# A hybrid attention and RWKV block on one core: the loads of the first norm reordered, the constants' broadcast copies spread, and a tile of its own for the last group's operand sums

## The chip, the cores and the metric

The kernel runs on one core of a Trainium2 chip. The metric is the device time of one execution in microseconds (us); the time before is the median of three runs. The core has a matrix engine (TensorE, PE in the profile), VectorE (DVE), ScalarE (ACT), GpSimd (POOL) and SyncE (SP), which here only issues DMA transfers. Each engine works through a queue of its own in order and waits on semaphores for the others. Operands lie in an on-chip memory of 128 partitions; TensorE writes to eight PSUM banks of 2 KB per partition. The language puts the instructions into the queues itself: a planner walks through the program with a cost model, and of the instructions that it takes to be ready puts first the one that comes first in the program. An order can be pinned by hand: `queue_behind(a, b)` sets a behind b in the queue of their engine, `keep_in_program_order(a)` sets a behind the instruction that the program has just before it on its engine; neither adds a wait.

## The reference, cut to what matters

One layer over 2048 rows of 1024 numbers, float32:

```python
h = rms_norm(x, pre_mix_g)
proj = h @ w_in                      # columns for attention q/k/v, RWKV r/k/v + low-rank w/a/g, gates
y_a = chunk_band_attention(q, k, v, rel_bias)     # own chunk of 64 and 8 chunks before, learned bias
y_b = rwkv7_time_mix(p_rwkv, shift_mu, w0, w2, a0, a2, g2, ...)
merged = sigmoid(gate_a) * (y_a @ proj_a) + sigmoid(gate_b) * (y_b @ proj_b)
x = x + rms_norm(merged @ w_out, post_mix_g)
u = square(relu(rms_norm(x, pre_ffn_g) @ w_up)) @ w_down
x = x + rms_norm(u, post_ffn_g)
```

## The kernel before, in words

Products keep float32 accuracy with operands in two parts: `split` (L69) rounds a tile to the matrix engine's format on ScalarE (hi, the "cast" below) and takes the rest on VectorE (lo, L71); `mm3` (L74) then issues three matmuls for each block of 128 in the contraction: hi by hi, hi by lo, lo by hi. Here whi and wlo are the weights' parts, hh and hl those of the normed rows.

The rows are taken in four groups of 512 (`G`), each of four tiles of 128 (`GT`). `run` (L1416) first starts the constants (memsets, identity), then the norm of group 0 in `phase_norm` (L285), then the rest of the constants, and then for each group `phase_rwkv`, `phase_attention` and `phase_merge`; after that the feed-forward part runs in two halves.

The norm of a tile (`norm_tile`, L315): a square with a sum on ScalarE (L319), the root in two steps on GpSimd (`rstd`, L102), a scale by root and gain on VectorE (L321), eight 128 by 128 transposes on TensorE into two PSUM banks, and from each bank a cast on ScalarE (L130) and a low part on VectorE (L131). The pool of these banks has two buffers. The program has the gain (g_pre) loaded ahead of the rows x. The order of the four tiles' steps on each engine is the planner's.

The second part of `constants` (from L199) loads the small parameter rows (L203) and the low-rank weights (L210), transposes the rows on TensorE (L212), splits the low-rank weights, and calls `build_bias` (L950). That one loads the relative biases, extends them on VectorE (ext), writes them to DRAM (band, L961), and copies the band of each of eight heads 128 times into DRAM with a shifted row length (skew, eight copies of 384 KB, L963); attention later reads its bias tiles from there. Eight further small copies (x0, L229) fill the start value of the inverse in RWKV. All of them are issued by SP.

A dense product of 128 columns (`dense`, L93) loads its 512 KB of weights over SP (`wsplit`, L58; two raw buffers), splits them, and issues 24 matmuls of 128 by 512. In group 0 the first is block 12 (`lora_wa`), the next are blocks 0, 4 and 8, that is r, k and v of the first pair of heads (`rwkv_pre`, L377). `rwkv_pre` calls `between()` at eight places, where the products of the gates are put in; `bias_corners` (L974) then overwrites corners of skew.

In `phase_merge` (L1044) eight products of the attention output are gated and added (th, mb), and then `w_out` is applied: two halves n, in each eight blocks k over four tiles t, which end in four PSUM banks ps_o; each bank is squared on ScalarE (L1080) and scaled into o on VectorE (L1081). Beside the first half run the steps of a generator (`beside`), one at each of k = 2, 4, 5, 6, 7: the load of four 256 KB tiles cmb (L1149), four subtractions in place on VectorE (L1121), and the stores (wd, L1145). These are operand sums for the feed-forward part. `run` puts cmb into a pool p1, ahead of the pools p0 and mo (o, g_post, sqo).

After the last group `mixing` is closed, and its memory goes to the feed-forward pools in the order z, b, raw and so on. `first_half` (L1161) loads bl (L1166) and splits it into bh and bl; `phase_up` follows. A tile that takes the memory of an earlier one waits for the last use of that one.

Of the kernel before, what the change touches and what calls it, by code (L numbers as in the profile page):

```python
# [9 lines left out]
F32 = mybir.dt.float32  # L10
# [3 lines left out]
ALU = mybir.AluOpType  # L14
# [36 lines left out]
class Block:  # L51
# [5 lines left out]

    def wsplit(self, src, tag, k, n, raw_tag="raw", bufs=2):  # L58

        nc = self.nc  # L60
        w = self.wp
        raw = w.tile([P, k, n], F32, tag=raw_tag, name="wraw")
        nc.sync.dma_start(raw, src)
        hi = w.tile([P, k, n], F32R, tag=tag + "h", bufs=bufs, name="whi")
        lo = w.tile([P, k, n], F32R, tag=tag + "l", bufs=bufs, name="wlo")
        self.split(hi, lo, raw)
        return hi, lo

    def split(self, hi, lo, src):  # L69
        high = self.nc.scalar.copy(hi, src)  # L70
        self.nc.vector.tensor_tensor(lo, src, hi.bitcast(F32), ALU.subtract)  # L71
        return high.ins

    def mm3(self, ps, terms):  # L74

        nc = self.nc
        n, last, mm = 0, 3 * len(terms) - 1, []
        for lh, ll, rh, rl in terms:
            for l, r in ((lh, rh), (lh, rl), (ll, rh)):
                mm.append(nc.tensor.matmul(ps, l, r, start=n == 0, stop=n == last).ins)  # L80
                n += 1
        return mm
# [5 lines left out]
    def blocks_behind(self, *places):  # L88

        for ins, i in zip(self.blocks, places):  # L90
            self.queue_behind(ins, self.mm[i])

    def dense(self, col):  # L93

        wh, wl = self.wsplit(
            self.a["w_in"][:, col : col + P].rearrange("(k p) n -> p k n", p=P), "w", KB, P
        )
        ps = self.pd.tile([P, G], F32, tag="d", name="psd")
        self.mm = self.mm3(ps, [(wh[:, k], wl[:, k], self.h[0][:, k], self.h[1][:, k]) for k in range(KB)])
        return ps  # L100

    def rstd(self, pool, ssq, scale, eps, post=None):  # L102
        nc = self.nc
        v = pool.tile([P, 1], F32, tag="rs_v", bufs=4, name="rs_v")
        nc.gpsimd.tensor_scalar(v, ssq, scale, eps, ALU.mult, ALU.add)
        r = pool.tile([P, 1], F32, tag="rs_r", bufs=4, name="rs_r")
        nc.gpsimd.tensor_tensor(r, v, self.nhalf[:, 0:1], ALU.pow)  # L107
# [11 lines left out]
    def transpose_split(self, pt, src, hi, lo, tok, pinned=False):  # L119

        nc = self.nc
        for h in range(2):
            ps = pt.tile([P, 4, P], F32, tag="tr", name="pstr")
            for j in range(4):
                k = h * 4 + j
                mm = nc.tensor.transpose(ps[:, j], src[:, k * P : (k + 1) * P], self.ident)
                if pinned and j == 0:
                    self.tc.keep_in_program_order(mm)
            hv, lv = hi[:, h * 4 : h * 4 + 4, tok], lo[:, h * 4 : h * 4 + 4, tok]
            nc.scalar.copy(hv, ps)  # L130
            nc.vector.tensor_tensor(lv, ps, hv.bitcast(F32), ALU.subtract)  # L131


    def constants(self, ctx, mixing):
# [57 lines left out]
        with tc.tile_pool(name="setup", bufs=1, side="right") as sp, \  # L192
# [18 lines left out]
            ps = pp.tile([P, nrow], F32, name="ps_rows")  # L211
            nc.tensor.transpose(ps, raw, self.ident[:nrow, :nrow])  # L212
            nc.vector.tensor_copy(self.cst, ps)

            for par in range(2):
                r = slice(par * C, par * C + C)
                nc.scalar.copy(self.wh[par], raw2[par])
                o = slice(C - par * C, P - par * C)
                nc.vector.memset(self.wl[par][o].bitcast(F32), 0.0)
                nc.vector.tensor_tensor(  # L220
                    self.wl[par][r], raw2[par][r], self.wh[par][r].bitcast(F32), ALU.subtract
                )
            self.build_bias(sp, dp)
            eyeb = sp.tile([2, 512], BF16, name="eyeb")
            nc.vector.tensor_copy(eyeb, eye.rearrange("p r j -> p (r j)"))
            eyed = dp.tile([2, 512], BF16, name="eyed")
            nc.sync.dma_start(eyed, eyeb)
            for i in range(8):
                nc.sync.dma_start(  # L229
                    self.x0[i * 16 : i * 16 + 16].rearrange("p r j -> p (r j)"),  # L230
                    eyed[i % 2][None, :].to_broadcast((16, 512)),
                )

# [50 lines left out]

    def phase_norm(self, g, sp, pt, ahead=2):  # L285

        self.h = self.alloc_h()
        gt = self.gain(sp, self.a["pre_mix_g"], "g_pre", ahead if ahead == 2 else 1)
        for t in range(GT):
            x = sp.tile([P, D], F32, tag="x", bufs=ahead, name="x")  # L290
            self.nc.sync.dma_start(x, self.a["x"][g * G + t * P : g * G + (t + 1) * P])
            self.norm_tile(sp, pt, x, gt, *self.h, slice(t * P, (t + 1) * P), ahead)
            yield

# [20 lines left out]
    def norm_tile(self, sp, pt, x, gt, hi, lo, tok, ahead=2, pinned=False):  # L315
        nc = self.nc
        xn = sp.tile([P, D], F32, tag="xn", bufs=ahead, name="xn")
        ssq = sp.tile([P, 1], F32, tag="ssq", bufs=4, name="ssq")
        nc.scalar.activation(xn, x, AF.Square, accum_out=ssq)  # L319
        r = self.rstd(sp, ssq, 1.0 / D, RMS_EPS)  # L320
        nc.vector.scalar_tensor_tensor(xn, x, r, gt, op0=ALU.mult, op1=ALU.mult)  # L321
        self.transpose_split(pt, xn, hi, lo, tok, pinned)


# [391 lines left out]
    def phase_rwkv(self, g, quads):  # L716
        tc = self.tc
        with ExitStack() as ctx:
# [230 lines left out]

    def build_bias(self, sp, dp):  # L950

        nc = self.nc

        self.skew = dp.tile([8, P * 769], F32, name="skew")
        band = dp.tile([8, 768], F32, name="band")
# [3 lines left out]
        nc.vector.tensor_scalar(ext[:, 383:703], ext[:, 383:703], -1.0, None, ALU.mult)  # L959
        nc.vector.tensor_copy(ext[:, 0:383], ext[:, 383:384].to_broadcast((8, 383)))  # L960
        nc.sync.dma_start(band, ext)  # L961
        for h in range(8):
            nc.sync.dma_start(  # L963
                self.skew[h].rearrange("(q m) -> q m", m=769)[:, 0:768], band[h][None, :].to_broadcast((P, 768))
            )

    def load_bias(self, h):
# [76 lines left out]
    def phase_merge(self, g, o, op, between, beside):  # L1044

        tc, nc, a = self.tc, self.nc, self.a
        with ExitStack() as ctx:
# [13 lines left out]
            for n in range(2):  # L1061
                ps = [po.tile([P, 512], F32, tag="o", name="ps_o") for _ in range(GT)]
                for k in range(KB):
# [3 lines left out]
                    for t in range(GT):  # L1067
                        ts = slice(t * P, (t + 1) * P)
                        for j, (l, r) in enumerate(((mh, wh), (mh, wl), (ml, wh))):
                            nc.tensor.matmul(  # L1070
                                ps[t], l[:, k, ts], r[:, k % 2], start=k == 0 and j == 0, stop=k == KB - 1 and j == 2
                            )
                    if n == 0 and k in (2, 4, 5, 6, 7):
                        advance(beside, 1)
# [341 lines left out]
    def run(self):  # L1416
        tc, e = self.tc, None
        with ExitStack() as ctx, ExitStack() as mixing:
# [90 lines left out]
```

## Time and profile before

| what | value |
|---|---|
| median of 3 runs | 3300.28 us (3299.59 to 3302.99) |
| profiled execution | 3302.74 us, of it the span from first to last instruction 3301.0 us |
| TensorE busy | 3189.4 us, 97% of the span |
| VectorE, ScalarE, GpSimd busy | 68%, 48%, 18% |
| transfers | 592.53 MB, 179 GB/s over the span |
| granted TensorE clock, mean | 0.992 |

How to read it: a row of the timeline gives start and length in us, engine, line, operation, the tile written, an arrow, the tiles read, shapes, and in brackets how long the engine stood idle before it and who ended that. SPq and POOLq stand for issuing a transfer, not for the transfer. A row of the waits gives who waited, for whom, the total in us, how often, and the longest. A row of the windows gives a stretch, then for each of PE, PEld (weight load), DVE, ACT and POOL the busy time, then the granted clock, the share of time in which the transfer engines were busy, and GB/s.

### The profile page before, as it was taken

To read this page: it belongs to the slowest core of one execution; us is meant where nothing else is said; L and a number is where in the kernel's file an instruction comes from. 1 tells how busy PE (TensorE), PEld (TensorE's weight loads), DVE (VectorE), ACT (ScalarE), POOL (GpSimd) and SP (SyncE) were. 2 spreads that over 40 slices of the span, in tenths; PEclk is the share of its full clock that TensorE was granted. 3 is DMA by queue.
4 is the path that set the end of the run, shared out by engine and by line. 5 is a ranking of instruction groups with operands and counts; after the bars stand their busy time and mean duration, and the time that the engine had idled before them with its cause. 6 is when DMAs were issued, how large, how long until landed. Compare 5 with 4: busy or idle time off the path is not lost. (4 is left out here: it accounts for less than half of the span.)

```text
span 3301.0 us, 49967 instructions
## 1 busy us (share of the span) xinstructions
PE 3189.4 (97%) x18913; PEld 2601.3 (79%) x18913; DVE 2245.6 (68%) x3655; ACT 1570.8 (48%) x2511; POOL 595.8 (18%) x1093
## 2 busy tenths in 40 slices
PE   7999999999999999999999999999999999999998
PEld 5777778778877777878777887878788878888887
DVE  5875766785766875776876775777656667775455
ACT  3434634434744434754444654544543454454343
POOL 2222012222102222111232110122211112220000
PEclk9999999999999999999999999999999999999999
DMA  5335473247564236555326647654787875546665
GB/s 152 90 110 185 129 239 118 81 131 240 170 223 150 87 108 222 189 194 185 96 76 201 200 155 234 231 179 153 248 291 239 285 248 190 170 161 235 193 215 178
DMA packets 432281, 592.53 MB, mean 179 GB/s; under 512 B 25300, under 2 KB 295840, under 8 KB 432040
## 3 DMA queue, kind: packets, MB, share of 16 engines
q1 hardware_dynamic: 375080, 413.14, 40.0%
q0 software_dynamic: 47744, 159.42, 13.1%
q10 hardware_dynamic: 9216, 16.78, 1.4%
q8 instruction: 149, 2.44, 0.3%
q14 instruction: 92, 0.75, 0.1%
HBM read 425.37 MB, written 167.01 MB: 179 GB/s over the span
## 5 line engine op out<-in xcount | busy, mean ns | idle before, releaser
L1345 PE MATMUL ps_dn<-fop 128*128 128x512 f32 x2688 | 611.8, 389 | 2.9 <-DVE fop L71 2.9
L1345 PEld LDWEIGHTS ps_dn<-fop 128*128 128x128 f32 x2688 | 503.9, 188 | 108.9 <-DVE fop L71 4.3
L80 PE MATMUL psd<-hh,whi 128*128 128x512 f32 x1344 | 541.4, 403 | 10.7 <-ACT whi L70 7.0
L80 PE MATMUL psd<-hl,whi 128*128 128x512 f32 x1344 | 542.4, 404 | 0.0
L80 PE MATMUL psd<-hh,wlo 128*128 128x512 f32 x1344 | 538.5, 401 | 2.6 <-DVE wlo L71 2.6
L70 ACT CAST whi<-wraw 128x1024 fp32r<-128x1024 f32 x232 | 243.3, 1049 | 424.1 <-PE psd L80 329.9
L71 DVE TENSOR_TENSOR wlo<-wraw,whi 128x1024 fp32r<-128x1024 f32 x232 | 282.9, 1220 | 165.9 <-ACT whi L70 139.1
L80 PEld LDWEIGHTS psd<-hh,whi 128*128 128x128 f32 x1344 | 255.9, 190 | 62.1 <-ACT whi L70 7.9
L80 PEld LDWEIGHTS psd<-hh,wlo 128*128 128x128 f32 x1344 | 256.1, 191 | 55.9 <-DVE wlo L71 5.1
L80 PEld LDWEIGHTS psd<-hl,whi 128*128 128x128 f32 x1344 | 256.5, 191 | 48.9
L71 DVE TENSOR_TENSOR fop<-xraw,fop 128x1024 fp32r<-128x1024 f32 x112 | 137.0, 1223 | 166.7 <-ACT fop L70 165.9
L70 ACT CAST fop<-xraw 128x1024 fp32r<-128x1024 f32 x112 | 117.8, 1052 | 244.9 <-PE ps_dn L1345 178.5
L1227 POOL DMA_DIRECT2D xd<-X x192 | 103.8, 541 | 394.3 <-ACT X L1224 339.5
L71 DVE TENSOR_TENSOR fop<-wdraw,fop 128x1024 fp32r<-128x1024 f32 x112 | 136.6, 1220 | 26.6 <-ACT fop L70 26.1
L70 ACT CAST fop<-wdraw 128x1024 fp32r<-128x1024 f32 x112 | 117.7, 1051 | 42.8 <-DMA wdraw<-in_w_down_dram 29.8
L903 DVE CUSTOM_DVE_ANT_0 sc<-bias,ps_s 128x640 f32<-128x640 f32 (+4 forms) x128 | 93.8, 732 | 54.0 <-PE ps_pt L914 32.2
L908 ACT ACTIVATE sc<-sc,mn 128x640 f32<-128x640 f32 (+4 forms) x128 | 97.7, 764 | 45.2 <-DVE mn L903 44.8
L70 ACT CAST s12h<-s 128x1024 fp32r<-128x1024 f32 x32 | 33.7, 1054 | 165.0 <-PE ps_u L80 165.0
L80 PE MATMUL ps_p<-yh,whi 128*128 128x512 f32 x256 | 101.3, 405 | 7.5 <-DVE th L1041 3.8
L1070 PE MATMUL ps_o<-whi,mh 128*128 128x512 f32 x256 | 101.6, 397 | 6.1 <-DVE o L1081 6.1
L919 DVE TENSOR_TENSOR PTl<-ps_pt,PTh 128x640 fp32r<-128x640 f32 (+4 forms) x128 | 94.2, 736 | 18.7 <-ACT PTh L918 17.2
L1070 PE MATMUL ps_o<-wlo,mh 128*128 128x512 f32 x256 | 100.6, 393 | 3.2 <-DVE wlo L71 3.2
(368 smaller groups left out, 6826.1 us busy)
## 6 DMA issues: line engine op xcount, KB each, us to landing
wraw<-in_w_in_dram SPq DMA_DIRECT2D x168, 512.0 KB
xraw<-xd SPq DMA_DIRECT2D x112, 512.0 KB
xd<-X POOLq DMA_DIRECT2D x192, 256.0 KB, 5.2
wraw<-in_w_up_dram SPq DMA_DIRECT2D x80, 512.0 KB
wdraw<-wd SPq DMA_DIRECT2D x64, 512.0 KB
wdraw<-in_w_down_dram SPq DMA_DIRECT2D x48, 512.0 KB
gd<-gate ACTq DMA_DIRECT2D x64, 256.0 KB
wd<-cmb POOLq DMA_DIRECT2D x64, 256.0 KB, 3.7
```

Of the source, the lines that this page charges most:

```text
L70: high = self.nc.scalar.copy(hi, src)
L71: self.nc.vector.tensor_tensor(lo, src, hi.bitcast(F32), ALU.subtract)
L80: mm.append(nc.tensor.matmul(ps, l, r, start=n == 0, stop=n == last).ins)
L903: nc.vector.tensor_tensor_reduce(sc[:, 0:n], bias[:, s0:640], pss[:, c0 : c0 + n], 1.0, 3.0e38, ALU.add, ALU.min, mn,)
L908: nc.scalar.activation(sc[:, 0:n], sc[:, 0:n], AF.Exp, scale=-1.0, bias=mn, accum_out=sm[:, col : col + 1])
L919: nc.vector.tensor_tensor(lv, pst[:, 0:nk], hv.bitcast(F32), ALU.subtract)
L1070: nc.tensor.matmul(ps[t], l[:, k, ts], r[:, k % 2], start=k == 0 and j == 0, stop=k == KB - 1 and j == 2)
L1227: nc.gpsimd.dma_start(self.xd[q][i // 2][:, i % 2], src)
L1345: nc.tensor.matmul(ps, o[:, l, k, sl], o[:, r, k], start=start and n == 0, stop=stop and n == end)
```

## The change

Group 0 gets a norm of its own, `first_norm`, in place of `phase_norm`. It loads the first tile of x, the gain, the other three tiles, and then the weights of the first two dense products (blocks 12 and 0), all ahead of the constants' loads. It orders the tiles' steps by hand: root behind the root before, from tile 2 on the square behind the last cast of the tile two before it, and the scale behind the low part of that tile. The bank pool of the transposes gets four buffers. In `dense` the first two products take the raw weights that are there; their casts are queued behind the last cast of tile 1 and of tile 2, their low parts behind the norm's last low part, their first matmul behind the last transpose; and their 24 matmuls go by part: the eight of hi by hi, then the eight of hi by lo, then the eight with wlo.

The constants' VectorE work and the row transpose are queued behind the norm's. The eight x0 and the eight skew copies move out of the constants into a generator `spread`, of which one step is taken at each `between()` of the first two `rwkv_pre` of group 0.

In the last group a pad takes the place of cmb in p1, and cmb comes from a new pool p2, opened after mo; the steps of `beside` there come at k = 0, 2, 3, 4, 5.

```diff
+    def load_raw(self, src, k, n):
+        raw = self.wp.tile([P, k, n], F32, tag="raw", name="wraw")
+        self.nc.sync.dma_start(raw, src)
+        return raw
...
     def wsplit(...):
-        raw = w.tile([P, k, n], F32, tag=raw_tag, name="wraw")
-        nc.sync.dma_start(raw, src)
+        raw = self.raws.pop(0) if self.raws else self.load_raw(src, k, n)
...
     def mm3(self, ps, terms, by_part=False):
-        for lh, ll, rh, rl in terms:
-            for l, r in ((lh, rh), (lh, rl), (ll, rh)):
-                mm.append(nc.tensor.matmul(ps, l, r, start=n == 0, stop=n == last).ins)
-                n += 1
+        pairs = [((lh, rh), (lh, rl), (ll, rh)) for lh, ll, rh, rl in terms]
+        for l, r in chain(*(zip(*pairs) if by_part else pairs)):
+            mm.append(nc.tensor.matmul(ps, l, r, start=n == 0, stop=n == last).ins)
+            n += 1
...
     def dense(self, col):
+        first = bool(self.raws)
+        wh, wl = self.wsplit(self.w_in(col), "w", KB, P)
+        if first:
+            self.queue_behind(self.high.ins, self.highs[2 - len(self.raws)])
+            self.queue_behind(self.low, self.last_low)
         ps = self.pd.tile([P, G], F32, tag="d", name="psd")
+        self.mm = self.mm3(ps, [...], first)
+        if first:
+            self.queue_behind(self.mm[0], self.last_transpose)
...
     def constants(self, ctx, mixing):
-            nc.tensor.transpose(ps, raw, self.ident[:nrow, :nrow])
-            nc.vector.tensor_copy(self.cst, ps)
+            self.queue_behind(nc.tensor.transpose(ps, raw, self.ident[:nrow, :nrow]).ins, self.last_transpose)
+            behind = lambda x: self.queue_behind(x.ins, self.last_low)
+            behind(nc.vector.tensor_copy(self.cst, ps))
...
-            for i in range(8):
-                nc.sync.dma_start(
-                    self.x0[i * 16 : i * 16 + 16].rearrange("p r j -> p (r j)"),
-                    eyed[i % 2][None, :].to_broadcast((16, 512)),
-                )
+            self.eyed = eyed
...
+    def first_norm(self, sp, pt):
         self.h = self.alloc_h()
+        xs = []
         for t in range(GT):
+            xs.append(sp.tile([P, D], F32, tag="x", bufs=GT, name="x"))
+            self.nc.sync.dma_start(xs[t], self.a["x"][t * P : (t + 1) * P])
+            if t == 0:
+                gt = self.gain(sp, self.a["pre_mix_g"], "g_pre")
+        self.raws = [self.load_raw(self.w_in(RW0 + blk * P), KB, P) for blk in (12, 0)]
+        steps = []
+        for t in range(GT):
+            steps.append(self.norm_tile(sp, pt, xs[t], gt, *self.h, slice(t * P, (t + 1) * P), GT))
+            square, root, scaled = steps[t][:3]
+            if t:
+                self.queue_behind(root[0], steps[t - 1][1][1])
+            if t > 1:
+                self.queue_behind(square, steps[t - 2][3])
+                self.queue_behind(scaled, steps[t - 2][4])
+        self.highs = [x[3] for x in steps]
...
     def phase_rwkv(self, g, quads):
+            spread = self.spread() if g == 0 else iter(())
             def places(plan, act):
                 it = iter(plan)
-                return lambda: act(next(it, 0))
+                def between():
+                    act(next(it, 0))
+                    advance(spread, 1)
+                return between
...
             Rs = [self.rwkv_pre(g, q, rp, NA, between) for q in range(2)]
+            advance(spread)
             if g == 0:
                 self.bias_corners()
...
     def build_bias(self, sp, dp, behind):
+        behind(nc.vector.tensor_scalar(ext[:, 383:703], ext[:, 383:703], -1.0, None, ALU.mult))
         nc.vector.tensor_copy(ext[:, 0:383], ext[:, 383:384].to_broadcast((8, 383)))
         nc.sync.dma_start(band, ext)
+    def spread(self):
+        dma = self.nc.sync.dma_start
+        for i in range(8):
+            dma(
+                self.x0[i * 16 : i * 16 + 16].rearrange("p r j -> p (r j)"),
+                self.eyed[i % 2][None, :].to_broadcast((16, 512)),
+            )
+            yield
         for h in range(8):
-            nc.sync.dma_start(
-                self.skew[h].rearrange("(q m) -> q m", m=769)[:, 0:768], band[h][None, :].to_broadcast((P, 768))
+            dma(
+                self.skew[h].rearrange("(q m) -> q m", m=769)[:, 0:768],
+                self.band[h][None, :].to_broadcast((P, 768)),
             )
+            yield
...
     def phase_merge(...):
-                    if n == 0 and k in (2, 4, 5, 6, 7):
+                    if n == 0 and k in ((2, 4, 5, 6, 7) if g + 1 < self.NG else (0, 2, 3, 4, 5)):
                         advance(beside, 1)
...
     def run(self):
-                 tc.tile_pool(name="p0p", bufs=2, space=PSUM, reuse_waits="tile") as pt:
-                advance(self.phase_norm(0, sp, pt, GT))
+                 tc.tile_pool(name="p0p", bufs=4, space=PSUM, reuse_waits="tile") as pt:
+                self.first_norm(sp, pt)
             advance(consts)
...
                     cmb = c.enter_context(tc.tile_pool(name="p1", bufs=1, reuse_waits="tile"))
+                    if g + 1 == self.NG:
+                        cmb.tile([P, 4 * G], F32, tag="pad", name="pad")
                     sp = c.enter_context(tc.tile_pool(name="p0", bufs=2, reuse_waits="tile"))
...
                     op = c.enter_context(tc.tile_pool(name="mo", bufs=1, reuse_waits="tile"))
+                    if g + 1 == self.NG:
+                        cmb = c.enter_context(tc.tile_pool(name="p2", bufs=1, reuse_waits="tile"))
                     b = cmb.tile([P, 4, G], F32, tag="cmb", name="cmb")
```

`split`, `rstd`, `transpose_split` and `norm_tile` only hand out the instructions that are named above; the splits of the low-rank weights in the constants are wrapped in `behind` as well.

More of the change, by code (lines that the diff above doesn't have):

```diff
@@ L91, in blocks_behind, with w_in @@
             self.queue_behind(ins, self.mm[i])
+    def w_in(self, col):
+        return self.a["w_in"][:, col : col + P].rearrange("(k p) n -> p k n", p=P)
     def dense(self, col):
-        wh, wl = self.wsplit(
-            self.a["w_in"][:, col : col + P].rearrange("(k p) n -> p k n", p=P), "w", KB, P
-        )
+        first = bool(self.raws)
[3 more added lines that the diff above has]
+            self.queue_behind(self.low, self.last_low)
         ps = self.pd.tile([P, G], F32, tag="d", name="psd")
-        self.mm = self.mm3(ps, [(wh[:, k], wl[:, k], self.h[0][:, k], self.h[1][:, k]) for k in range(KB)])
+        self.mm = self.mm3(ps, [(wh[:, k], wl[:, k], self.h[0][:, k], self.h[1][:, k]) for k in range(KB)], first)
+        if first:
+            self.queue_behind(self.mm[0], self.last_transpose)
         return ps
@@ L104, in rstd @@
         v = pool.tile([P, 1], F32, tag="rs_v", bufs=4, name="rs_v")
-        nc.gpsimd.tensor_scalar(v, ssq, scale, eps, ALU.mult, ALU.add)
+        v_ins = nc.gpsimd.tensor_scalar(v, ssq, scale, eps, ALU.mult, ALU.add)
         r = pool.tile([P, 1], F32, tag="rs_r", bufs=4, name="rs_r")
-        nc.gpsimd.tensor_tensor(r, v, self.nhalf[:, 0:1], ALU.pow)
+        r_ins = nc.gpsimd.tensor_tensor(r, v, self.nhalf[:, 0:1], ALU.pow)
+        self.roots = v_ins.ins, r_ins.ins
         if post is not None:
@@ L129, in transpose_split @@
             hv, lv = hi[:, h * 4 : h * 4 + 4, tok], lo[:, h * 4 : h * 4 + 4, tok]
-            nc.scalar.copy(hv, ps)
-            nc.vector.tensor_tensor(lv, ps, hv.bitcast(F32), ALU.subtract)
+            self.last_high = nc.scalar.copy(hv, ps).ins
+            self.last_low = nc.vector.tensor_tensor(lv, ps, hv.bitcast(F32), ALU.subtract).ins
     def constants(self, ctx, mixing):
@@ L219, in constants @@
                 nc.vector.memset(self.wl[par][o].bitcast(F32), 0.0)
-                nc.vector.tensor_tensor(
+                behind(nc.vector.tensor_tensor(
                     self.wl[par][r], raw2[par][r], self.wh[par][r].bitcast(F32), ALU.subtract
-                )
-            self.build_bias(sp, dp)
+                ))
+            self.build_bias(sp, dp, behind)
             eyeb = sp.tile([2, 512], BF16, name="eyeb")
@@ L318, in norm_tile @@
         ssq = sp.tile([P, 1], F32, tag="ssq", bufs=4, name="ssq")
[L319 removed]
+        square = nc.scalar.activation(xn, x, AF.Square, accum_out=ssq)
         r = self.rstd(sp, ssq, 1.0 / D, RMS_EPS)
[L321 removed]
+        scaled = nc.vector.scalar_tensor_tensor(xn, x, r, gt, op0=ALU.mult, op1=ALU.mult)
         self.transpose_split(pt, xn, hi, lo, tok, pinned)
+        return square.ins, self.roots, scaled.ins, self.last_high, self.last_low
     def mix(self, g, blk, out):
@@ L948, in finish, with build_bias @@
         self.split(self.ya[0][:, p], self.ya[1][:, p], ya)
-    def build_bias(self, sp, dp):
+    def build_bias(self, sp, dp, behind):
         nc = self.nc
         self.skew = dp.tile([8, P * 769], F32, name="skew")
-        band = dp.tile([8, 768], F32, name="band")
+        band = self.band = dp.tile([8, 768], F32, name="band")
         ext = sp.tile([8, 768], F32, name="ext")
```

17 lines of the change are left out of this document (5 added, 12 removed).

## The prediction, made before the changed kernel was run

> **What bounds the kernel now.** I read the page first, then the waits of TensorE over the whole run, then the timeline of the two places where its long waits lie.
>
> ```profile
> span 3301.0 us, 49967 instructions
> PE 3189.4 (97%) x18913; PEld 2601.3 (79%) x18913; DVE 2245.6 (68%) x3655; ACT 1570.8 (48%) x2511; POOL 595.8 (18%) x1093
> ```
> ```profile
> PE pstr L126 <- DVE xn L321: 10.4, 1, 10.4
> PE psd L80 <- ACT whi L70: 7.0, 2, 5.4
> PE ps_o L1070 <- DVE o L1081: 6.1, 1, 6.1
> ```
>
> TensorE (PE) is busy for 97% of the span, so what counts is the time in which it has nothing to do, or runs slowly. Three waits stand out: 10.4 us before its first instruction, one of 5.4 us for weights of a dense product, one of 6.1 us in a merge. All three lie where the diff is: the first two in the first 46 us, the third in the last group's merge. The timeline of the start, several engines mixed:
>
> ```profile
> 5.48 0.25 SPq L203 DMA_DIRECT2D rows<-in_a_dram  x1
> 6.72 0.25 SPq L203 DMA_DIRECT2D rows<-in_k_k_dram  x1
> 6.72 1.06 ACT L319 ACTIVATE xn<-x 128x1024 f32<-128x1024 f32 x1 [4.65 <-DMA x<-in_x_dram]
> 8.45 0.56 POOL L107 TENSOR_TENSOR rs_r<-rs_v,nhalf 128x1 f32<-128x1 f32 x1
> 9.04 1.28 DVE L321 SCALAR_TENSOR_TENSOR xn<-x,rs_r,g_pre 128x1024 f32<-128x1024 f32 x1 [3.66 <-POOL rs_r L107]
> 10.38 1.97 PE L126 MATMUL pstr<-ident,xn 128*128 128x128 f32 x8 [10.38 <-DVE xn L321]
> 16.77 0.69 DVE L131 TENSOR_TENSOR hl<-pstr,hh 128x512 fp32r<-128x512 f32 x1
> 22.38 0.59 ACT L130 CAST hh<-pstr 128x512 fp32r<-128x512 f32 x1
> 22.86 1.99 ACT L70 CAST whi<-wraw 128x1024 fp32r<-128x1024 f32 x2
> 23.96 0.79 PE L80 MATMUL psd<-hh,whi 128*128 128x512 f32 x1 [1.62 <-ACT whi L70]
> 24.26 0.27 SPq L961 DMA_DIRECT2D band<-ext  x1
> 24.99 2.36 DVE L71 TENSOR_TENSOR wlo<-wraw,whi 128x1024 fp32r<-128x1024 f32 x2
> 26.27 0.79 PE L80 MATMUL psd<-hh,wlo 128*128 128x512 f32 x1 [1.08 <-DVE wlo L71]
> 26.82 5.45 SPq L963 DMA_DIRECT2D skew<-band  x8
> 27.28 0.63 PE L80 MATMUL psd<-hl,whi 128*128 128x512 f32 x1
> 27.71 0.63 PE L80 MATMUL psd<-hh,wlo 128*128 128x512 f32 x1
> 31.98 0.39 PE L80 MATMUL psd<-hh,whi 128*128 128x512 f32 x1
> 32.21 0.39 PE L80 MATMUL psd<-hl,whi 128*128 128x512 f32 x1
> 36.23 35.05 SPq L63 DMA_DIRECT2D wraw<-in_w_in_dram  x7
> 44.89 1.04 ACT L70 CAST whi<-wraw 128x1024 fp32r<-128x1024 f32 x1 [0.86 <-DMA wraw<-in_w_in_dram]
> 45.99 0.80 PE L80 MATMUL psd<-hh,whi 128*128 128x512 f32 x1 [5.41 <-ACT whi L70]
> 52.50 0.40 PE L80 MATMUL psd<-hh,wlo 128*128 128x512 f32 x1
> ```
>
> Two spacings are to be seen. From 27.28 to 27.71 one dense matmul takes 0.43 us; from 31.98 to 32.21 it takes 0.23. TensorE runs at half speed until 31.98, and again from 45.99 to 52.50, after it had idled for 5.41 us. So a long wait costs twice. The 5.41 us themselves come from SyncE's queue (SP): the weights of the third dense block (k) are issued at 36.23 only, behind the band and eight skew copies, and, with those copies in front of them in the transfers, their cast starts at 44.89. Why the copies start at 26.82 the waits of SP in the first 50 us say:
>
> ```profile
> SPq L961 <- DVE ext L960: 6.7, 1, 6.7
> SPq L203 <- DMA x<-in_x_dram: 4.0, 4, 1.0
> ```
>
> The second line also dates the input: the tiny row loads wait each for a landing eight issues back, so those at 5.48 and 6.72 show g_pre and the first tile of x landed, one 512 KB load every 1.24 us.
>
> The third wait, in the last group's merge (waits of SP around it, then the timeline, then a window):
>
> ```profile
> SPq L1166 <- DMA wd<-cmb: 7.0, 2, 6.3
> ```
> ```profile
> 2015.18 0.54 POOL L1145 DMA_DIRECT2D wd<-cmb  x1 [0.19 <-issue]
> 2021.65 0.34 SPq L1166 DMA_DIRECT2D bl<-ht  x1
> 2025.44 1.04 ACT L1158 CAST bh<-bl 128x1024 fp32r<-128x1024 f32 x1 [6.24 <-DMA bl<-ht]
> 2027.66 1.28 DVE L1081 TENSOR_TENSOR o<-ps_o,g_post 128x512 f32<-128x512 f32 x2
> 2028.39 0.80 PE L1070 MATMUL ps_o<-whi,mh 128*128 128x512 f32 x1 [6.07 <-DVE o L1081]
> 2032.30 0.39 PE L1070 MATMUL ps_o<-whi,ml 128*128 128x512 f32 x1
> ```
> ```profile
> 2000.00:2010.00 10.00, 10.00 (x46) 8.29 (x45) 6.63 (x9) 3.88 (x5) 0.40 (x1) 1.00 1.13 324
> ```
>
> The operand bl of the next phase takes the memory in which the sums (cmb) lay: by the tile sizes, cmb stands behind the weights (24 KB) and h (32 KB) at 56 to 64 KB, bl behind z (32 KB) and bh (16 KB) at 48 to 64 KB. So bl's load waits 6.3 us for the stores of the sums; ScalarE stands at bl's cast until 2025.44, the evacuation of ps_o is queued behind it, and TensorE lacks a bank for 6.07 us.
>
> **The change, part by part.** The profiled run took 3302.74 us (span 3301.0 and 1.74 around it), 2.46 above the median of 3300.28; each saving below is taken from both alike.
>
> *The first norm.* From the start of a square to the transposes are 10.38 - 6.72 = 3.66 us. With x ahead of g_pre the first tile lands at 5.48, and transposes start at 9.1 (the scale needs g_pre, which now lands at 6.72, well before 7.8). Tile 1 lands near 8.0 and transposes at 11.7. The square of tile 2 is queued behind tile 0's second cast: 9.1 + 1.97 + 0.59 = 11.7, transposes at 15.4, with a low part of 0.69 likely in front on VectorE. The square of tile 3 follows tile 1's casts, at 11.7 + 1.97 + 0.59 = 14.3, transposes near 17.9, and the last cast ends 17.9 + 1.97 + 0.59 = 20.4. Four PSUM banks for the transposes let none of them wait. The first weights, now ahead of the rows, land after x as loads six and seven, near 13, and their first cast (1.0 us) fits between the squares. So the first dense product starts at 20.4.
>
> In before it starts at 23.96, but its third matmul waits for wlo until 26.27: a steady series would have begun two half-speed spacings earlier, at 25.4. Ordered by part, the first 16 matmuls (6.9 us at half speed, to 27.3) need no wlo, which is due by 20.4 + 0.69 + 1.2 = 22.3, and even behind all the constants' copies on VectorE before 27. Gain 25.4 - 20.4 = 5.0 us; at least 1.5 if the norm ends as now, at most 7.
>
> *The stall for weights.* The buffer of the third load is free when the first wlo is done, near 22.3. Band may still stand before it on SP, since its source is queued behind the norm's last low part; that makes it 24 or 25. With transfers as slow as now (44.89 - 36.23 = 8.7 us) its cast starts at 33 or 34, without the copies in front earlier. The product is due at 20.4 + 12 x 0.43 + 36 x 0.23 + four lora matmuls of 0.23 = 34.8. That is in time: 5.4 us go (0 if the copies still precede the weights). With it goes the second slow stretch: 14 matmuls from 45.99 to 52.50 take 6.5 us where 14 x 0.23 = 3.2 would do, 3.3 us.
>
> *The slow stretch that stays.* From 25.4 to 31.98 it is 6.6 us; after the merge's wait it was 3.9 (2028.39 to 2032.30). I take the middle, 5.2: half of 1.4 less, 0.7 us (0 to 1.4). [...]
>
> *The spread copies.* Eight small and eight skew copies now stand between the steps of the first two heads' preparation. Place in the program is only priority to the planner that fills the queues, so the skew copies may still come out in a block once band has landed; but the third and fourth weights now go first. Later weights pass them in the queue of transfers:
>
> ```profile
> 90.00:100.00 10.00, 10.00 (x46) 8.25 (x45) 5.77 (x7) 6.08 (x10) 2.55 (x5) 1.00 0.27 79
> ```
>
> There the transfers use 0.27 of their time and TensorE is full: room for one copy of about 2 us (some 15 us of transfers for all sixteen, by 26.82 to 44.89 less two weight loads) beside each load. I take 0, at worst 3 us. The corner stores wait for the last copy on SP, with weights queued behind; two raw buffers cover that.
>
> *Does it reach the end?* In that row VectorE is at 5.77 of 10 and waits for TensorE's products, so its chain moves forward with them. I count the whole 5.0 + 5.4 + 3.3 + 0.7 = 14.4 us.
>
> *The sums' own tile.* A pad holds the old place, which no instruction touches; the sums lie behind the merge's output tiles, and their steps come one to two k earlier. The wait of 6.3 us for the stores vanishes. At stake are 6.07 us and the slow stretch behind it (nine matmuls in 3.91 us instead of 2.05): 7.9. But the transfers are full there (1.13 in the window): bl's 2 MB and the sums' 1 MB must pass earlier, among the loads that the merge needs. I take 6.0, from 0 to 7.9.
>
> Sum: 14.4 + 6.0 = 20.4 us. The profiled run becomes 3282.3, the median **3279.9**.
>
> **Rivals.** *The merge only swaps its wait.* Free since the attention, bl is loaded as soon as SP has time, ahead of th, mb and the weights; the full window speaks for it, TensorE's two spare banks against. If bl comes behind what is queued and lands 3 us earlier than now, a gap of 3.1 us and its slow stretch stay, and 3.0 are gained; if it pushes others back, none. 3300.3 - 14.4 - 0 to 3 = 3283 to 3286. [...]
>
> *The copies still precede the third weights.* If the planner puts band and the skew copies first, issue slips to about 32 and the cast to 41, so most of the 5.4 and 3.3 stays: 3300.3 - 5.0 - 0.7 - 6.0 = 3288.6. Against: the new order leaves them behind in priority.
>
> *Slower.* Spread out, each skew copy sits before a weight load, and SP, which issues in order, waits at it. If a copy and the wait for its completion slot made every load late by over its cover, each of eight loads would leave a gap of the 5.4 + 3.3 = 8.7 us kind: from four such gaps on (35 us against 20.4) the kernel is slower, near 3315. Against it: transfers at 0.27.
>
> *It does nothing.* The planner keeps its order and the merge a wait: 3297 to 3302.
>
> **How the numbers follow.** Forecast 0.57, merge swap 0.20, copies first 0.12, nothing 0.07, slower 0.04. 0.2% is 6.6 us, about what a measurement of this kernel can tell. The first three are faster by more than that: 0.89; same 0.07; slower 0.04. The range goes from all bounds at their best (7 + 5.4 + 3.3 + 1.4 + 7.9 = 25, and 2 for later waits) to the third case with 1.4 added: 3273 to 3290.
>
> **What would show it.** First dense matmul near 20.4, its first 16 all on whi; no wait for whi over 1 us before 60; one slow stretch; the k weights issued before any skew copy; L1166 without a wait for wd<-cmb and no wait of ps_o over 3 us. It is wrong if a gap of over 3 us stands anywhere in the first 120 us after the dense products begin, or if the third product starts after 38.

## The result and the profile after

| what | before | after |
|---|---|---|
| median of four runs each, side by side | 3299.94 us (3299.13 to 3302.99) | 3286.01 us (3281.66 to 3288.77) |
| profiled execution, its span | 3302.74, 3301.0 us | 3286.72, 3285.0 us |
| TensorE busy | 3189.4 us | 3184.0 us |

The ratio is 0.9947 (95% interval 0.9934 to 0.9959). Of 3299.94 us that is 13.5 to 21.8 less; the two medians, 13.9 us apart, lie at the small end. The kernel is faster. The medians show less than the 20.4 us of the forecast; the interval of these runs still holds 20.4, that of the six further runs below doesn't.

The page of the changed kernel first, and then TensorE's waits in it, in the first 120 us and around the last merge (who waited, for whom, us in total, times, longest):

```profile
span 3285.0 us, 49969 instructions
PE 3184.0 (97%) x18913; PEld 2599.8 (79%) x18913; DVE 2246.0 (68%) x3655; ACT 1569.2 (48%) x2511; POOL 593.7 (18%) x1093
```
```profile
PE pstr L139 <- DVE xn L343: 11.4, 4, 8.3
PE ps_bonus L511 <- ACT rh L75: 1.0, 1, 1.0
```
```profile
PE ps_o L1113 <- DVE o L1124: 2.7, 1, 2.7
PE ps_p L85 <- DVE th L1084: 1.8, 2, 1.4
```

The waits for weights at the start are gone. The wait of ps_o is 2.7 us instead of 6.1, and a wait for th (the gate tiles of the merge's first products) has come in front of it. The timeline of the start, several engines mixed:

```profile
4.63 1.06 ACT L341 ACTIVATE xn<-x 128x1024 f32<-128x1024 f32 x1 [2.56 <-DMA x<-in_x_dram]
8.30 1.97 PE L139 MATMUL pstr<-ident,xn 128*128 128x128 f32 x8 [8.30 <-DVE xn L343]
17.32 1.94 PE L139 MATMUL pstr<-ident,xn 128*128 128x128 f32 x8 [1.06 <-DVE xn L343]
19.12 3.65 PE L85 MATMUL psd<-hh,whi 128*128 128x512 f32 x8
19.30 0.59 ACT L144 CAST hh<-pstr 128x512 fp32r<-128x512 f32 x1 [0.27 <-PE pstr L139]
22.61 1.99 PE L85 MATMUL psd<-hl,whi 128*128 128x512 f32 x8
23.83 2.34 DVE L76 TENSOR_TENSOR wlo<-wraw,whi 128x1024 fp32r<-128x1024 f32 x2
25.10 1.52 SPq L61 DMA_DIRECT2D wraw<-in_w_in_dram  x2
26.02 1.98 PE L85 MATMUL psd<-hh,wlo 128*128 128x512 f32 x8
29.13 1.05 ACT L75 CAST whi<-wraw 128x1024 fp32r<-128x1024 f32 x1
31.68 0.39 PE L85 MATMUL psd<-hh,whi 128*128 128x512 f32 x1
32.52 1.17 SPq L1004 DMA_DIRECT2D skew<-band  x2
```

Eight matmuls take 3.65 us at 19.12 and 1.99 at 22.61: the half-speed stretch is 3.5 us long and is the only one at the start. It is read from this spacing; the profile's clock column has 1.00 there. The third block's weights are issued at 25.10, before any skew copy, and are cast 2.5 us before their product starts at 31.68 (45.99 before).

Now ScalarE and TensorE in the last merge, and the window that holds the long wait:

```profile
2000.71 1.05 ACT L75 CAST s3h<-wraw 128x1024 fp32r<-128x1024 f32 x1 [3.41 <-DMA wraw<-in_w_up_dram]
2001.67 1.04 ACT L75 CAST whi<-wraw 128x1024 fp32r<-128x1024 f32 x1
2002.73 0.60 ACT L1123 ACTIVATE sqo<-ps_o 128x512 f32<-128x512 f32 x1
```
```profile
1971.63 0.50 PE L85 MATMUL ps_p<-yh,whi 128*128 128x512 f32 x1 [1.44 <-DVE th L1084]
...
2004.81 0.50 PE L1113 MATMUL ps_o<-whi,mh 128*128 128x512 f32 x1 [2.72 <-DVE o L1124]
```
```profile
2000.00:2010.00 10.00, 7.28 (x26) 5.50 (x25) 5.89 (x7) 5.35 (x11) 0.00 (x0) 0.83 1.09 304
```

ScalarE stands 3.41 us at a cast of feed-forward weights that haven't landed; the squares that empty the banks of ps_o are queued behind it. The transfers have no time left (1.09 in the last line), and the clock is 0.83: a gap of 2.72 us still cost 3.4 us at half speed (2005.6 to 2009.1). In the kernel before, the clock stood at half for twice as long at this wait, 6.8 us (2025.3 to 2032.2; TensorE was idle in it until 2028.39).

TensorE does the same 18,913 matmuls in both kernels, so the starts of the k-th one can be set side by side. The difference to the kernel before says where time goes (us, below zero is ahead; the second column of the changed kernel is another profiled execution, told of below; the start part alone and the merge part alone are the first two experiments):

| up to | after | after, second | start part alone | merge part alone |
|---|---|---|---|---|
| 100th matmul | -16.7 | -17.0 | -17.0 | -1.9 |
| last merge begins (13,250th) | -19.3 | -18.3 | -21.2 | -0.2 |
| just ahead of the ps_o wait (13,400th) | -17.7 | -16.9 | -20.4 | +5.6 |
| past the ps_o wait (13,450th) | -21.2 | -22.5 | -19.0 | -1.5 |
| before the first down phase (14,900th) | -20.9 | -22.5 | -19.4 | -0.8 |
| 100 matmuls on (15,000th) | -15.6 | -19.9 | -18.5 | -0.4 |
| last matmul | -15.9 | -21.1 | -18.5 | +1.6 |

The gain of the start is in by the 100th matmul; between there and the merge single profiles drift by up to 4.2 us ahead or 2.6 behind. The merge first loses 1.6 us and then gains 3.5, net 1.9. A further 5.3 us are lost at the first down phase, which the change doesn't touch.

### The profile page after: what moved, and what is told of

Read it like the earlier page. It is cut to its first block, busy times and chain, and to the rows that moved or that the text cites. A ratio compares the mean times of both kernels' runs of the same rounds, so it can differ in the third digit from the quotient of the medians.

```text
span 3285.0 us, 49969 instructions
## 1 busy us (share of the span) xinstructions
PE 3184.0 (97%) x18913; PEld 2599.8 (79%) x18913; DVE 2246.0 (68%) x3655; ACT 1569.2 (48%) x2511; POOL 593.7 (18%) x1093
```

## The experiments

### The two parts alone

The start part alone is the changed kernel with the old merge; the merge part alone is the kernel before with the new one.

```diff
# start part alone, against the changed kernel
-                    if n == 0 and k in ((2, 4, 5, 6, 7) if g + 1 < self.NG else (0, 2, 3, 4, 5)):
+                    if n == 0 and k in (2, 4, 5, 6, 7):
-                    if g + 1 == self.NG:
-                        cmb.tile([P, 4 * G], F32, tag="pad", name="pad")
...
-                    if g + 1 == self.NG:
-                        cmb = c.enter_context(tc.tile_pool(name="p2", bufs=1, reuse_waits="tile"))
```

> The change without its last part: in the last group's merge the operand sums lie and step as before. Theory A (the start is worth about 16.5 us, the merge about 2): 3283 to 3285, that is 15 to 17 us under before; the wait of ps_o for o is near 6 us again and the clock halves for two windows behind it. Theory B (the merge is worth the 6 us of the prediction, and the start correspondingly less or given back by the later stages): 3288 to 3291. The first 60 us look as in the changed kernel in both.

> The kernel before with the last part of the change alone: the sums' own tile and their earlier steps in the last group. Theory A: 1 to 3 us under before, with a wait of ps_o of 2 to 3 us left and ps_p waiting 1 to 2 us for th that it did not wait for before. Theory B: 5 to 7 us under before, no wait of ps_o over 1 us.

The two windows of the first theory A are two stretches of 3.4 us: the 6.8 us at half speed that the kernel before has at this wait. Start part alone: 3284.86 us, ratio 0.9956 (0.9940 to 0.9971). Merge part alone: 3302.3 us, 1.0006 (0.9996 to 1.0015). So the start part is the whole measurable gain, and the merge part by itself is worth between 5 us lost and 1.3 gained; 6.0 lies outside. TensorE's waits in the last merge, start part alone and then merge part alone, with a window of the latter:

```profile
PE ps_o L1113 <- DVE o L1124: 6.6, 1, 6.6
```
```profile
PE ps_p L80 <- DVE th L1041: 2.5, 2, 2.3
...
PE ps_o L1070 <- DVE wlo L71: 0.9, 1, 0.9
PE ps_o L1070 <- DVE o L1081: 0.7, 1, 0.7
```
```profile
1990.00:2000.00 10.00, 8.52 (x30) 6.92 (x31) 8.72 (x13) 3.13 (x5) 0.00 (x0) 0.83 0.82 267
```

The wait of ps_o goes nearly away, and TensorE loses in its place 2.5 us to th, with the clock at 0.83 after the longer of the two gaps. In the table it falls back 5.8 us before it gains 7.1. Neither theory holds as it stands: of the 1 to 3 us of theory A the interval leaves only the low end open, and the wait of ps_o for o is 0.7 us, not 2 to 3.

### The changed kernel again

> The changed kernel as it is, in more runs, to be held against the kernel with the start part alone (ratio to the kernel before 0.9956, 0.9940 to 0.9971). Theory, the merge part gives back nearly all that it gains (0 to 2 us): a ratio of 0.9945 to 0.9960, 3282 to 3287 us. Rival, the merge part is worth the 6.0 us of the prediction and one half of it was hidden in the scatter of the four first runs: a ratio at or below 0.9938, 3280 us or less.

3287.48 us (3281.56 to 3290.85, six runs), ratio 0.9961 (0.9947 to 0.9974). The mean of all ten runs of the changed kernel is 3286.5, that of the six with the start part alone 3285.9: in whole runs the merge part cannot be told from nothing, though their scatter (some 3 to 6 us from run to run) leaves several us open. The ratio lies just above the 0.9960 of the theory, and the interval excludes the rival's 0.9938. Part of the scatter is the clock: of the six runs with the start part alone the fastest, 3278.81 us, had a mean granted clock of 0.995, the slowest, 3296.37 us, one of 0.990, and 0.005 of such a run is some 16 us, an estimate from these two figures. The profiled execution of this set, 3281.56 us, is the second column of the table. Its wait and its window, beside 2.72 us and 0.83 of the first:

```profile
PE ps_o L1113 <- DVE o L1124: 2.2, 1, 2.2
```
```profile
2000.00:2010.00 10.00, 7.80 (x35) 6.11 (x34) 5.89 (x7) 5.36 (x11) 0.00 (x0) 1.00 1.09 299
```

The same program, a gap shorter by half a microsecond, and the clock stayed up: the merge nets 4.2 us here and 1.9 there.

### The new tile and the new steps apart

```diff
# new tile, old steps
-                    if n == 0 and k in ((2, 4, 5, 6, 7) if g + 1 < self.NG else (0, 2, 3, 4, 5)):
+                    if n == 0 and k in (2, 4, 5, 6, 7):
# old tile, new steps: the pad and the pool p2 are taken out instead
```

> The changed kernel with the sums' own tile but their steps at the old places (2, 4, 5, 6, 7). Theory A (the tile alone takes away the wait for the stores; the earlier steps only bring the loads of the sums among those of th): no wait of SP for the stores of the sums, waits for th under 1 us, ps_o waiting 1 to 3 us; the changed kernel's time or up to 2 us less. Theory B (the earlier steps are needed): ps_o waits over 4 us.

> The changed kernel with the earlier steps of the sums but their tile in the old place. Theory A (the wait for the stores stays but ends earlier, since the stores are issued some 5 us earlier): bl's load waits for the stores 1 to 4 us, ps_o waits under 4 us; within 2 us of the changed kernel. Theory B (the tile is what counts): ps_o waits near 6 us as in the kernel before.

New tile: 3283.76 us, 0.9948 (0.9934 to 0.9961). New steps: 3286.98 us, 0.9959 (0.9944 to 0.9974). The waits of TensorE with the new tile, and those of TensorE and SP with the old one:

```profile
PE ps_p L85 <- DVE th L1084: 2.8, 2, 2.4
PE ps_o L1113 <- DVE o L1124: 1.0, 1, 1.0
```
```profile
PE ps_u L85 <- ACT bh L1201: 3.4, 1, 3.4
PE ps_o L1113 <- DVE o L1124: 2.6, 1, 2.6
```
```profile
SPq L1209 <- DMA wd<-cmb: 8.2, 2, 7.5
```

The tile is what removes the wait for the stores; the steps alone leave it at 8.2 us and TensorE waits further on, at ps_u. The wait for th comes with the tile, whichever steps stand beside it. Matmul by matmul (13,250th to 13,450th) the merge nets 2.8 us ahead with the new tile and 2.2 behind with the old one. The other profiles say the same: all eight in this document that have the new tile and no further order by hand in the merge net between 0.0 and 4.2 us ahead of the kernel before, 2.6 on the mean, and the two with the new start and the old tile 2.2 behind. So the tile gains something in the merge itself; the whole times can't separate the two.

### What pushes th back, and what is left at ps_o

Two causes were argued. The loads of bl and of the sums, free of their wait, are issued among the last th loads (bl at 1962.82 and the sums from 1968.20, the last th at 1977.66) and share nearly full transfers with them (0.93 of their time from 1962 to 1978). And the splits of the feed-forward weights stand on ScalarE ahead of the squares. One kernel queues the loads behind the last th load, one the first three splits behind the squares and scales of ps_o, one does both.

```diff
# loads behind th
+        self.last_th = nc.sync.dma_start(t, self.gd[br * KB + i]).ins
...
+            if g == 0:
+                self.queue_behind(load.ins, self.last_th)      # bl; likewise the sums
# splits behind the banks
+                if n == 0:
+                    self.evac, self.npin = (sqi.ins, oi.ins), 3
...
+                if self.npin:
+                    self.npin -= 1
+                    self.queue_behind(self.high.ins, self.evac[0])
+                    self.queue_behind(self.low, self.evac[1])
```

> The changed kernel, with the first three splits of w_up queued behind the evacuation of the first half's banks in the last merge (casts behind the last square, low parts behind the last o). Theory A (what is left of the wait is the cast of the w_up block that stands before the squares on ScalarE and waits for its load): the wait of ps_o falls from 2.7 us to under 0.5, no slow window there, 3 to 4 us less than the changed kernel. Theory B (the full transfers set it, and whatever stands there waits): the wait moves to the weights of the second half, and the time is as in the changed kernel within 1 us.

> The changed kernel with the loads of bl and of the sums in the last group queued behind the last load of th, the w_up splits where the planner puts them. Theory A: the waits for th (1.8 us in the changed kernel) go, the wait of ps_o stays at 2 to 5 us, since bl's and w_up's splits still stand before the evacuation; time as in the changed kernel within 2 us. Theory B: ps_o waits over 6 us again and the whole gain in the merge is gone.

> The changed kernel with the first three w_up splits behind the evacuation of the banks, as in the run before, and besides in the last group the loads of bl and of the sums queued behind the last load of th. Theory A (the early loads of bl and of the sums push back the loads of th, and that is the 2 to 4 us that the merge loses ahead of ps_o): no wait of ps_p for th over 0.7 us, the wait of ps_o under 1 us, 1.5 to 3 us less than with the splits moved alone. Theory B (the transfers are full: what is loaded later is late later): a new wait, of ps_o for weights or of the first w_up product, and no gain over the splits moved alone.

TensorE's waits there: splits behind the banks, loads behind th, both.

```profile
PE ps_p L88 <- DVE th L1087: 2.7, 2, 2.0
```
```profile
PE ps_o L1117 <- DVE o L1128: 3.7, 1, 3.7
PE ps_p L88 <- DVE th L1087: 0.9, 2, 0.6
```
```profile
PE ps_o L1117 <- DVE wlo L79: 0.6, 1, 0.6
PE ps_p L88 <- DVE th L1087: 0.4, 1, 0.4
```

Each pin takes away all or most of the wait that it was made for and leaves the other: with the splits moved, ps_o doesn't wait at all (the merge nets 5.7 us); with the loads moved, th costs 0.9 and ps_o 3.7 (net 1.7); with both, 1.0 us is left of all (net 7.2). These are single profiles, but in the seven with the new start (whole, or but for a piece or two), the new tile and no pin, th costs 1.4 to 3.3 us and ps_o waits 1.0 to 2.7 for o, more in each than where the pin stands. The two causes are shown for the waits in the merge. The times are 3281.38 us, 0.9940 (0.9926 to 0.9954), for the splits; 3287.67, 0.9960 (0.9946 to 0.9973), for the loads; 3280.67, 0.9941 (0.9928 to 0.9955), for both. The first and the last are the fastest measured, but their intervals overlap with the changed kernel's. That both pins did no better than one in the whole run, though they did in the merge, was not followed up.

### The start, piece by piece

Four kernels undo one thing each: the copies back in the constants; the first two products by block instead of by part; the norm's steps in the planner's order; and that with two banks.

```diff
# copies early: the sixteen copies stand in constants and build_bias again
-            spread = self.spread() if g == 0 else iter(())
+            spread = iter(())
# by block: `first` is not handed to mm3
# planner's order
-            if t:
-                self.queue_behind(root[0], steps[t - 1][1][1])
-            if t > 1:
-                self.queue_behind(square, steps[t - 2][3])
-                self.queue_behind(scaled, steps[t - 2][4])
# two banks: the line above, and p0p with bufs=2
```

> The changed kernel with the sixteen copies issued in the constants again, all else as changed. Theory A (place in the program is priority: the copies take SP and the transfers ahead of the third block's weights): a wait for the weights of the third block of 5 to 8 us and a second slow stretch, 7 to 11 us more than the changed kernel. Theory B (loading the first two blocks early frees the raw buffers early, so the third and fourth go first even so): no wait over 1 us, same time as the changed kernel.

> The changed kernel with the first two products' matmuls in the old order, hi by hi, hi by lo, lo by hi for each block. Theory A (VectorE does the constants before the first wlo, which comes near 25): the third matmul waits from 20 to 25, and the third product starts 3 to 5 us later than the changed kernel's. Theory B (the planner takes the first wlo earlier, since it is needed earlier): wlo done near 22, third product 1 to 2 us later.

> The changed kernel without the order by hand of squares, roots and scales in the first norm (four banks kept). Theory A (the order by hand counts): the first dense matmul 1 to 3 us later than 19.1, with roots behind scales on GpSimd. Theory B (x ahead of the gain, the early weights and four banks do it): within 0.5 us of 19.1.

> As the run without the order by hand, and with two PSUM banks for the transposes as before. Theory A (with the planner's order the low parts come late, and the transposes wait for them): first dense matmul 2 to 4 us later than 19.1. Theory B: within 1 us of the run with four banks.

| undone | time, us | ahead at the 100th matmul, us | third product starts |
|---|---|---|---|
| nothing | 3286.01 | 16.7 | 31.68 |
| copies early | 3297.14, ratio 0.9993 (0.9983 to 1.0002) | 1.5 | 45.38 |
| by block | 3293.01, one run | 11.0 | 36.87 |
| planner's order | 3288.83, one run | 14.6 | 34.29 |
| planner's order, two banks | 3281.55, one run | 14.6 | 34.30 |

One run says little of a time here (the last is below the changed kernel); the middle column does. The copies decide. Rows of that kernel's timeline, several engines mixed:

```profile
26.00 5.42 SPq L998 DMA_DIRECT2D skew<-band  x8
35.21 11.77 SPq L61 DMA_DIRECT2D wraw<-in_w_in_dram  x3
44.28 1.04 ACT L75 CAST whi<-wraw 128x1024 fp32r<-128x1024 f32 x1 [7.57 <-DMA wraw<-in_w_in_dram]
45.38 0.79 PE L85 MATMUL psd<-hh,whi 128*128 128x512 f32 x1 [11.31 <-ACT whi L75]
```

The norm is as early as in the changed kernel, and nearly all of it is lost: the weights are issued at 35.21, behind the copies, where the kernel before has 36.23, and TensorE waits 11.31 us instead of 5.41. The earlier start alone only lengthened the wait that follows. Against the changed kernel the cast at 44.28 is 15.2 us later: 10.1 of them the later issue, 5.0 the longer load, with eight copies of 384 KB issued just ahead of it. By block, the matmuls wait for wlo:

```profile
24.99 0.80 PE L85 MATMUL psd<-hh,wlo 128*128 128x512 f32 x1 [3.91 <-DVE wlo L76]
```

and the slow stretch lasts to 28.8 instead of 22.5, 5.7 us in all. Without the hand order the last transposes start at 19.23 instead of 17.32, and 2.1 us of the 16.7 are gone. With two banks besides, transposes wait for low parts, and the first dense product starts 0.8 us later than with four (first row: four banks; the others: two):

```profile
21.04 3.76 PE L85 MATMUL psd<-hh,whi 128*128 128x512 f32 x8
```
```profile
17.52 1.97 PE L139 MATMUL pstr<-ident,xn 128*128 128x128 f32 x8 [0.55 <-DVE hl L145]
21.87 3.02 PE L85 MATMUL psd<-hh,whi 128*128 128x512 f32 x8
```

That the third product starts at the same time even so is luck: the half-speed stretch happened to be shorter, 3.02 against 3.76 us for the first eight matmuls. With the hand order two banks were not tried.

## Why the prediction was right, and where it was not

The signs that the prediction named for itself all came, the last one narrowly: ps_o waits 2.7 us, under 3. Term by term it looks less even.

*The first dense product* was forecast at 20.4 and started at 19.12. The first square came at 4.63, not 5.48 as reckoned from before's row loads, and the product doesn't need the last cast: its first matmul uses the first half of the last tile (cast at 18.44), while the second half's cast runs from 19.30. So this term is 25.4 - 19.1 = 6.3 instead of 5.0.

*The stall for weights*: 5.4 gone, as forecast, with the issue at 25.10 (24 or 25) and the cast at 29.13 (33 or 34); with the copies behind it a load took at most 4 us, not 8.7. That the issue hit its forecast is partly luck. The prediction had the buffer free near 22.3 and band as what holds the weights up; but band is issued at 23.97, and SP then waits for the first wlo (waits of SP from 20 to 27):

```profile
SPq L61 <- DVE wlo L76: 1.5, 2, 0.8
```

VectorE comes to wlo at 23.83 only, behind the work for the constants. TensorE doesn't miss it, since seven hi by hi matmuls of the second product run first. *The second slow stretch*: 3.3, gone. *The first one* became 3.5 us instead of 5.2, worth 1.6 when the difference to 6.6 is halved as the prediction did, instead of 0.7. Sum 6.3 + 5.4 + 3.3 + 1.6 = 16.6, against 16.7 counted by matmuls. The size of this last term is chance: in the nine profiles with the same first norm and order by part the stretch lasts 1.7 to 3.5 us.

Part of this is the luck of the one profile of before. The merge part alone has the old start, and was 1.9 us ahead of that profile at its 100th matmul; against it the new start gains 14.8. The 14.4 of the forecast is just under what the start is worth, 14.8 to 16.7.

*The spread copies*: they come in groups of two, two and four between weight loads from 32.52 on, and no wait of TensorE over 1.0 us stands in the first 120 us after the norm. Their cost is the 0 that was taken. The slower rival, a gap at each load, has nothing in the profile. The rival with the copies first was priced by an issue near 32 and a cast at 41; the kernel built that way shows 35.21 and 44.28, so it was priced too kindly: at the start it keeps 1.5 us, not the 5.7 of that sum.

*The sums' own tile* is the step that failed in the whole runs: 6.0 us were counted. The wait of bl for the stores did vanish, as said, but the gain at ps_o (3.5 us in the first profile, 5.6 in the second, 7.1 with the merge part alone) is paid for beforehand, mostly at th (1.6, 1.4 and 5.8). That nets 1.9, 4.2 and 1.3 in the merge, against the one profile of before; against the start part alone, which itself nets 2.2 behind there, the first two are 4.1 and 6.4. Over whole runs of the part alone it is between 5 us lost and 1.3 gained, and why they show less than the merge does stays open. The prediction had named this as a rival, "the merge only swaps its wait", with bl ahead of th and a price of 3283 to 3286; the changed kernel, at 3286.01, and the waits in its merge fit that rival. That the total still lies in the forecast's range comes from a start that is as good as forecast or better. What the rival missed is the second cause, the splits ahead of the squares.

*The clock after a short gap.* The rival left a gap of 3.1 us its slow stretch. That is what shorter gaps did here, though not every time: 2.72 us (first profile) and 2.34 (merge part alone, 0.83 over 10 us) each cost 3.4 us at half speed, while 2.20 (second profile) and 2.53 (copies early, same place) cost none (1.00 over the windows around them). At the gaps of 5.41 and 6.07 us in the kernel before, the clock is at half for 6.8 us (45.6 to 52.4 and 2025.3 to 2032.2). But the length of the gap does not set that of the slow stretch, as the next paragraph shows.

*The rest*: the loss at the first down phase. A 512 KB load issued at 2346.89 was cast at 2358.97, 12.1 us later (before: 2367.75 and 2377.47, 9.7 us). The rows and a window of the changed kernel:

```profile
2358.97 1.04 ACT L75 CAST fop<-wdraw 128x1024 fp32r<-128x1024 f32 x1 [3.98 <-DMA wdraw<-in_w_down_dram]
2360.06 0.50 PE L1388 MATMUL ps_dn<-fop 128*128 128x512 f32 x1 [2.18 <-ACT fop L75]
```
```profile
2360.00:2370.00 10.00, 9.18 (x27) 7.05 (x28) 7.26 (x6) 7.22 (x9) 2.58 (x5) 0.66 0.83 253
```

The late load explains less than half of the 5.3 us: the gap is 2.18 us long, and behind it the clock stays at half for 6.8 us (0.66 over this window, 1.00 in the same place before), which costs 3.4. In the second profile it is a gap of 0.75 us, and behind it 22 matmuls from 2358.31 that take 6.89 us, where at a spacing of 0.23 they would take some 5.2; together that is 2.5 us, its loss.

The order of the queues there is that of before, and the kernel with the splits moved loses only 0.2 us in this place. It is taken for the scatter of one execution; why these two loads, under transfers that were full in both kernels (1.01 from issue to cast), took 12.1 and 9.7 us stays open.

## What to carry to other kernels

Starting the first products earlier was worth almost nothing here until the next load on the same queue was early too: of 16.7 us at the start, 15.2 hung on bulk copies that stood ahead of the third weights. The tile that no longer waited for its memory was loaded as soon as its queue was free, in front of what others needed sooner (bl was issued at 1962.82, the last th at 1977.66); give the freed load a place in the queue when the wait is taken away. And a difference of single profiles is worth no more than the scatter of the place: hold it against a second execution of the same program.

## What the runs showed of the hardware

The clock was lost after some gaps of 2 to 3 us, and not by length alone: 2.34 us (merge part alone) cost it for 3.4 us and 2.53 us (copies early) did not, and 2.18 us cost it for 6.8 us in the first down phase of the first profile. The same program in two executions had 2.72 and 2.20 us at the same wait, one with a slow stretch of 3.4 us and one without. A wait of this size was worth its own length, or 1.7 or 3.4 us more (half of 3.4 and of 6.8).
